# Down product of the second layer's MLP: tokens stationary, 512 columns of weights moving, in four groups of four units

## The chip, the cores and the metric

The kernel runs on one core of a Trainium2 chip. The metric is the device time of one execution in microseconds (us); lower is better. The engines are called as the profile calls them: PE is TensorE (matmuls; PEld is its weight load), DVE is VectorE, ACT is ScalarE, POOL is GpSimd, and SP is the queue that issues most transfers from memory.

## The reference

Two decoder layers over 512 tokens of width 1024. Each layer is RMS norm, attention with its input and output projections, residual, then RMS norm, an MLP and residual. Only the MLP of the second layer is touched:

```python
def squared_relu_mlp(h, w_up, w_down):
    u = jnp.einsum("bsd,df->bsf", h, w_up)
    return jnp.einsum("bsf,fd->bsd", jnp.square(jax.nn.relu(u)), w_down)

def reference(x, ...):
    for layer in range(DEPTH):
        ...
        h = rms_norm(x, g_mlp[layer])
        x = x + squared_relu_mlp(h, w_up[layer], w_down[layer])
    return x
```

All of it is float32: x is (1, 512, 1024), `w_up` 1024 x 4096 and `w_down` 4096 x 1024 in each layer.

## The kernel before, in words

**Precision.** Every float32 operand of a matmul is split into two parts, `hi` (a copy rounded to fp32r, made by ACT) and `lo` (the rest, a subtraction on DVE). A product is three matmuls: hi with hi, lo with hi, hi with lo (`mm3` and `mm_half`). So each 128x512 block of weights costs one ACT cast (`whi`, L763) and one DVE subtraction (`wlo`, L764) ahead of its matmuls.

**The MLP (function `mlp`, called with `last` for the second layer).** The 4096 hidden values are cut into 16 units of 256. An item ("U", u) computes unit u: four positions of 12 matmuls, each 128x512 (weights stationary, 512 tokens moving), then ReLU. After it `unit_end` squares the unit and prepares it for the down product.

**The down product.** It is done with seven block products in place of eight. The weights of an item are cut in quarters 11, 12, 21, 22 (first digit: half of the output columns, second digit: half of the hidden values), the activations in quarters b11 to b22 (half of the hidden values, half of the tokens). Sums of quarters (s1 to s4 of the weights, made in `ws`, L856; t1 to t4 of the activations, made in `t_sums`, L784) enter four of the products. `ORDER` lists them: (11, b11), (1, t1), (2, t2), (4, b22), (3, t3), (12, b21), (22, t4), with the PSUM bank X, Y or Z in which each is accumulated. An item ("D", g, dp) does all seven for group g of four units and for 256 output columns, so each group takes four items, dp 0 to 3, of 7 positions. A product is 4 x 3 matmuls with weights stationary and 256 tokens moving (L950, L953, L954), and one more matmul per item opens bank Y (L943). `combine` (L966) adds each bank to the residual `accs`, which lies with the channels on the partitions.

**The last unit.** In the second layer the fourth group holds three units (`NL = 1`), and unit 15 is done in `down_last` at the very end by plain products: 32 transposes bring `accs` into token order (L1109), ACT copies them scaled (L1113), then 48 matmuls with tokens stationary and 512 weight columns moving (L1118 to L1122), and DVE scales and adds (L1124) before the output is stored (L1125).

**The norm.** The MLP runs on activations that aren't normed yet. `mean_squares` forms v = mean of squares + eps in two layouts: along the free dimension (`ssum`, from a 128x512 matmul, L791) and along partitions (`r2col` = 1/v, L793). The residual is multiplied by v (`scale_residual`, eight DVE products, L799), and `down_last` multiplies everything by 1/v.

**The order.** The items stand in one list; each item is cut in positions, and at position n the loop issues the matmuls of n, `combine` of n-1, the cast of position n+6 (`prep`, R = 6; its subtraction follows one position later), the load of weights some positions further ahead (`early`), and whatever was put on that position by hand (`at`, `plan`, the tables FIN, FIND, FINL). Within the MLP the four engines' instructions are kept in this order (`PINS = 'pgva'`). There are 7 buffers each for `whi` and `wlo`, 4 for loaded weights (`wraw`, 512 KB each), 14 for split activations (`act`), and 4 + 4 PSUM banks (`pA`, `pB`). Items around a group: U(4g+4), then the four D items of group g, then U(4g+5) to U(4g+7).

Of the kernel before, what the change touches and what calls it, by code (L numbers as in the profile page):

```python
# [9 lines left out]
F32 = mybir.dt.float32  # L10
# [30 lines left out]
SCENG = ('vv', 'vv', 'vv', 'vv')  # L41
# [6 lines left out]
FINL = ((0, 0, 1, 1, 2), (8, 16, 16, 18, 20))  # L48
NL = 1
# [24 lines left out]
def trunk(ctx, tc, x, g_mix, g_mlp, w_in_even, a_q_gain, a_k_gain, b_q_gain, b_k_gain, b_sinks,  # L74
# [660 lines left out]
    def mlp(li, accs, attention_end, last):  # L735
# [5 lines left out]
        with ExitStack() as c2:  # L741
# [46 lines left out]
            def mean_squares():  # L788

                pr = bank("pB", "r2")  # L790
                tc.keep_in_program_order(nc.tensor.matmul(pr, ones, ssum, start=True, stop=True))  # L791
                if last:
                    vec(nc.vector.tensor_scalar(r2col, token_sums(ssum, True), 1.0 / D, EPS, op0=OP.mult, op1=OP.add))  # L793
                    vec(nc.vector.reciprocal(r2col, r2col))
                vec(nc.vector.tensor_scalar(ssum, pr, 1.0 / D, EPS, op0=OP.mult, op1=OP.add))
# [14 lines left out]
            NS = 3  # L810
            items = [("U", u) for u in range(4)]
            for g in range(NS):
                items.append(("U", 4 * g + 4))
                items += [("D", g, dp) for dp in range(4)]
                items += [("U", 4 * g + u) for u in range(5, 8)]
            items += [("D" if last else "E", NS, dp) for dp in range(4)]
            pos, first = [], []
            for j, it in enumerate(items):
                first.append(len(pos))
                pos += [(j, p) for p in range(7 if it[0] == "D" else 4)]  # L820
# [4 lines left out]
            def load(j):  # L825
                if j in raws or j >= len(items):
                    return
                it = items[j]
                raws[j] = [wp.tile([P, 4, 256], F32, tag="wraw", bufs=RAW, name="wraw") for _ in range(2)]
                for h in range(2):  # L830
                    if it[0] != "U":
                        src = wd[h, :, 4 * it[1]:4 * it[1] + nk(j), it[2] * 256:it[2] * 256 + 256]
# [3 lines left out]
                    nc.sync.dma_start(raws[j][h][:, :nk(j)], src)  # L836

            def nk(j):

                return 4 - NL if last and items[j][:2] == ("D", NS) else 4  # L840

            def quarter(j, q):
                return raws[j][q % 10 - 1][:, :nk(j), (q // 10 - 1) * P:(q // 10) * P]

            def ws(j, i):
# [5 lines left out]
                s = sums[j, i] = mp.tile([P, 4, P], F32, tag=f"s{i}", bufs=1, name="s")[:, :nk(j)]  # L851
# [13 lines left out]
            def early(n):  # L865

                if n < NP:
                    j, p = pos[n]
                    load(j)
                    if items[j][0] == "D" and ORDER[p][0] < 10:  # L870
                        ws(j, ORDER[p][0])

            def prep(n):
                if n >= NP:
                    return
                j, p = pos[n]
                if items[j][0] != "D":
# [6 lines left out]
                halves(hi[:, :nk(j)], lo[:, :nk(j)], src)  # L884
                ready[n] = hi, lo

            def up(j, p, hi, lo):

                if p % 2 == 0:
                    res[j, p] = bank(("pA", "pB")[j % 2], "up")  # L890
# [40 lines left out]
            def product(j, p, hi, lo):  # L931
# [13 lines left out]
                for k in range(nk(j)):  # L945
                    b = store[4 * it[1] + k][name]
                    mm_half(o, hi[:, k], lo[:, k], b, new and k == 0, k == nk(j) - 1, k == 0, not new)
# [20 lines left out]
            def unit_end(j):  # L968
# [8 lines left out]
                def whole(e):  # L977
                    s = slot("s") if u < 15 or last else mp.tile([P, 2, 512], F32R, tag="t24", bufs=2, name="s")
                    halves(s[:, 0], s[:, 1], v[:, e])
                    store[u, e] = s  # L980

                if last and u >= 16 - NL:
                    return [square, lambda: None, lambda: None, lambda: whole(0), lambda: whole(1)]
# [32 lines left out]

                return [square, tsum, b_part, lambda: t_part(0), lambda: t_part(1)]
# [6 lines left out]
            def plan(j):  # L1024
# [7 lines left out]
                else:  # L1032
                    offs = FINL[u - 15 + NL] if u >= 15 - NL else FIND if u % 4 == 0 and u else FIN
# [11 lines left out]
            for dp in range(4):  # L1045
                at(SCALE[dp], lambda dp=dp: scale_residual(dp, SCENG[dp]))
                if not last:
                    at(first[-7] + SC3[dp], lambda dp=dp: scale_residual(dp, "vv"))
            if not last:
                at(RPL, lambda: vec(nc.vector.reciprocal(ssum, ssum)))  # L1050

            def end(n):
# [3 lines left out]
                {"U": up_end, "D": combine, "E": direct_end}[items[j][0]](j, p)  # L1056
# [20 lines left out]
            for n, (j, p) in enumerate(pos):  # L1077
                early(n + R + LS)
                hi, lo = ready.pop(n)
                {"U": up, "D": product, "E": direct}[items[j][0]](j, p, hi, lo)  # L1080
# [11 lines left out]
            if last:  # L1092
                down_last(li, accs, [store[u, e] for u in range(16 - NL, 16) for e in range(2)], r2col)
# [3 lines left out]

    def down_last(li, accs, ss, r2col):

        r0 = FF // P - 2 * NL  # L1100
        for ch in range(2):
            cs = slice(ch * 512, (ch + 1) * 512)
            ws, rest = [], []
            for k in range(0, 2 * NL, 2):
                ws += load_w([(0, 0, w_down[li, (r0 + k) * P:(r0 + k + 2) * P, cs])], 512, 2, PAT_MLP)
            for m in range(4):
                pt = bank("pB", "fin")
                for c in range(4):
                    nc.tensor.transpose(pt[:, c * P:(c + 1) * P],  # L1109
                                        accs[2 * ch + c // 2][:, c % 2, m * P:(m + 1) * P], ident)  # L1110
                if m % 2 == 0:
                    rest.append(act.tile([P, 2, 512], F32, tag="act", name="rest"))
                nc.scalar.activation(rest[m // 2][:, m % 2], pt, AF.Copy, scale=r2col[:, m:m + 1])  # L1113
            for m in range(4):
                ts = slice(m * P, (m + 1) * P)
                o = bank("pA", "dn")
                for f in range(2 * NL):
                    mm = nc.tensor.matmul(o, ss[f][:, 0, ts], ws[f][0], start=f == 0, stop=False)  # L1118
                    if f == 0:
                        tc.keep_in_program_order(mm)  # L1120
                    nc.tensor.matmul(o, ss[f][:, 0, ts], ws[f][1], start=False, stop=False)
                    nc.tensor.matmul(o, ss[f][:, 1, ts], ws[f][0], start=False, stop=f == 2 * NL - 1)  # L1122
                a = rest[m // 2][:, m % 2]
                nc.vector.scalar_tensor_tensor(a, o, r2col[:, m:m + 1], a, op0=OP.mult, op1=OP.add)  # L1124
                nc.sync.dma_start(out[0, m * P:(m + 1) * P, cs], a)  # L1125
# [27 lines left out]
```

## Time and profile before

| what | value |
|---|---|
| median of 3 runs | 1192.4 us (1188.94 to 1193.04) |
| profiled execution, its time | 1192.98 us |
| span of its instructions | 1191.2 us, so 1.8 us lie around it |
| mean granted clock of TensorE | 0.995 of full |
| busy share: PE, DVE, ACT, POOL | 98%, 75%, 54%, 18% |
| MLP of the second layer | first matmul at 842.73 us, end at 1191.2 us |

A matmul's row shows when it started and its latency; matmuls are pipelined, so what one costs is the distance from its start to the next one's start.

### The profile page before, as it was taken

How to read it: one execution, taken by the hardware profiler on the slowest of the kernel's cores; microseconds unless marked ns; L12 is line 12 of the kernel's file. 1: busy time of each engine (PE TensorE's matmuls, PEld its weight loads, DVE VectorE, ACT ScalarE, POOL GpSimd, SP SyncE). 2: the span in 40 equal slices, each digit the busy share in tenths (PEclk: the TensorE clock that was granted, in tenths of full speed). 3: DMA queues.
4: the chain of work that ended last, by engine and by line, in shares of the span. 5: the costliest groups of instructions: out<-in, count | busy, mean ns of one | idle time of the engine just before them, and what ended most of it. 6: DMA issues, size and time to landing. Idle time of an engine off the chain costs nothing.

```text
span 1191.2 us, 18927 instructions
## 1 busy us (share of the span) xinstructions
PE 1162.3 (98%) x6902; PEld 1020.3 (86%) x6902; DVE 893.1 (75%) x1962; ACT 646.0 (54%) x1351; POOL 212.1 (18%) x307
## 2 busy tenths in 40 slices
PE   8799989999999999999999999999999999999998
PEld 7787887888888988988887888887889989889897
DVE  4987899878956947865657887878879578569585
ACT  6255876665445545444335675655655455455453
POOL 2445444200000000000155445432000000000000
PEclk9899999999999999999999999999999999999999
DMA  7342115232332332233443433343322423323322
GB/s 250 114 109 79 37 37 155 76 103 75 107 110 84 94 120 88 90 113 109 152 125 107 106 100 100 103 124 106 107 89 72 125 89 106 103 83 100 116 68 82
DMA packets 106197, 122.46 MB, mean 103 GB/s; under 512 B 6088, under 2 KB 95208, under 8 KB 106104
## 3 DMA queue, kind: packets, MB, share of 16 engines
q1 hardware_dynamic: 104920, 117.03, 32.3%
q0 software_dynamic: 576, 2.10, 0.5%
q10 hardware_dynamic: 608, 2.13, 0.4%
q8 instruction: 54, 0.88, 0.3%
q14 instruction: 39, 0.32, 0.1%
HBM read 108.10 MB, written 6.32 MB: 96 GB/s over the span
## 4 chain that ended last, share of the span: by engine, by line
PE 81%; DVE 10%; DMA 3%; issue 2%; ACT 2%; POOL 1%; SPq 0%; ACTq 0%; POOLq 0%; DVEq 0%
PE up L165 10%; PE up L168 10%; PE up L169 10%; PE pj L232 4%; PE pj L234 4%; PE pj L233 4%; PE Y L950 3%; PE Y L953 3%; PE Y L954 3%; PE O L383 2%; PE Z L950 2%; PE X L953 2%; PE X L950 2%; PE Z L954 2%; PE Z L953 2%; PE X L954 2%
## 5 line engine op out<-in xcount | busy, mean ns | idle before, releaser
L165 PE MATMUL up<-xin,whi 128*128 128x512 f32 x512 | 199.8, 390 | 0.0
L168 PE MATMUL up<-xin,wlo 128*128 128x512 f32 x512 | 199.3, 389 | 0.0
L169 PE MATMUL up<-xin,whi 128*128 128x512 f32 x512 | 199.2, 389 | 0.0
L763 ACT CAST whi<-wraw 128x512 fp32r<-128x512 f32 (+1 forms) x228 | 138.7, 613 | 106.4 <-PE up L169 48.3
L764 DVE TENSOR_TENSOR wlo<-wraw,whi 128x512 fp32r<-128x512 f32 (+1 forms) x228 | 152.1, 679 | 56.5 <-ACT whi L763 54.3
L169 PEld LDWEIGHTS up<-xin,whi 128*128 128x128 f32 x512 | 96.1, 188 | 20.1
L165 PEld LDWEIGHTS up<-xin,whi 128*128 128x128 f32 x512 | 96.1, 188 | 20.0 <-issue 0.2
L168 PEld LDWEIGHTS up<-xin,wlo 128*128 128x128 f32 x512 | 96.1, 188 | 19.9 <-issue 0.2
L763 ACT CAST whi<-s 128x512 fp32r<-128x512 f32 (+1 forms) x112 | 67.6, 604 | 70.0 <-PE Y L954 35.0
L343 ACT ACTIVATE P<-P,negm 128x128 f32<-128x128 f32 (+5 forms) x128 | 69.5, 544 | 52.9 <-DVE negm L340 51.0
L950 PE MATMUL Y<-t,whi 128*128 128x256 f32 x324 | 92.7, 286 | 3.0 <-DVE acc L966 2.6
L901 ACT ACTIVATE u<-up 128x512 f32<-128x512 f32 x64 | 38.3, 598 | 99.7 <-PE up L169 99.7
L953 PE MATMUL Y<-t,wlo 128*128 128x256 f32 x324 | 91.7, 283 | 0.0
L954 PE MATMUL Y<-t,whi 128*128 128x256 f32 x324 | 91.6, 283 | 0.0
L153 POOL TENSOR_SCALAR whi<-wraw 128x512 fp32r<-128x512 f32 x96 | 65.8, 687 | 140.7 <-PE pj L234 118.3
L232 PE MATMUL pj<-whi,hn 128*128 128x512 f32 (+2 forms) x256 | 88.7, 346 | 0.0
L234 PE MATMUL pj<-whi,hn 128*128 128x512 f32 (+2 forms) x256 | 86.9, 339 | 0.0
L233 PE MATMUL pj<-wlo,hn 128*128 128x512 f32 (+2 forms) x256 | 86.8, 339 | 0.0
L764 DVE TENSOR_TENSOR wlo<-s,whi 128x512 fp32r<-128x512 f32 (+1 forms) x112 | 73.7, 663 | 2.4 <-ACT whi L763 2.4
L232 PE MATMUL pj<-whi,h 128*128 128x512 f32 (+1 forms) x192 | 68.5, 361 | 6.9 <-DVE v L161 3.1
L156 POOL TENSOR_TENSOR wlo<-wraw,whi 128x512 fp32r<-128x512 f32 x52 | 69.7, 1344 | 21.8 <-ACT whi L151 18.7
L234 PE MATMUL pj<-whi,h 128*128 128x512 f32 (+1 forms) x192 | 66.6, 348 | 0.0
(200 smaller groups left out, 3138.6 us busy)
## 6 DMA issues: line engine op xcount, KB each, us to landing
wraw<-in_w_up SPq DMA_DIRECT2D x64, 512.0 KB, 3.8
wraw<-in_w_down SPq DMA_DIRECT2D x58, 512.0 KB, 4.0
wraw<-in_w_in_odd SPq DMA_DIRECT2D x36, 256.0 KB, 3.0
K<-K SPq DMA_DIRECT2D x26, 256.0 KB
wraw<-in_w_in_even SPq DMA_DIRECT2D x10, 512.0 KB, 4.4
wraw<-in_w_in_even SPq DMA_DIRECT2D x16, 256.0 KB, 4.4
xl<-xsp SPq DMA_DIRECT2D x8, 512.0 KB
bias<-csp SPq DMA_DIRECT2D x16, 256.0 KB, 3.5
```

Of the source, the lines that this page charges most:

```text
L156: in_order((nc.gpsimd if lo == "pool" else nc.vector).tensor_sub(dst_l, src, dst_h.bitcast(F32)))
L165: m = nc.tensor.matmul(o, wh, xh, start=start, stop=False, skip_group_check=more)
L168: nc.tensor.matmul(o, wl, xh, start=False, stop=False, skip_group_check=more)
L169: nc.tensor.matmul(o, wh, xl, start=False, stop=stop, skip_group_check=more)
L232: nc.tensor.matmul(o, xh, hi[:, :n], start=k == 0, stop=False)
L233: nc.tensor.matmul(o, xh, lo[:, :n], start=False, stop=False)
L234: nc.tensor.matmul(o, xl, hi[:, :n], start=False, stop=k == DC - 1)
L763: sca(nc.scalar.copy(dst_h, src))
L764: late.append(lambda: vec(nc.vector.tensor_sub(dst_l, src, dst_h.bitcast(F32))))
L950: m = nc.tensor.matmul(o, wh, b(0), start=start, stop=False, skip_group_check=more)
L953: nc.tensor.matmul(o, wl, b(0), start=False, stop=False, skip_group_check=more)
L954: nc.tensor.matmul(o, wh, b(1), start=False, stop=stop, skip_group_check=more)
```

## The change

In the second layer alone, the down product is turned round. An item ("T", g) now does group g for all 1024 output columns: a weight quarter is 512 columns wide, and the products have 128 tokens stationary and 512 weight columns moving. Each of the seven products has four positions (one for each unit k of the group), and a position is 2 token blocks x 3 matmuls of 128x512. Result banks hold tokens on the partitions, so `combine_t` adds a bank, multiplied by `r2col`, to `rest`, the residual in token order. The 32 transposes for `rest` move from the end to positions 11 to 18 (in U2 to U4), four at each position, unscaled. The fourth group takes all four units, with unit 15's preparation put right behind it (`FIN15`), and `down_last` is gone, as are `scale_residual` and the 128x512 matmul of `mean_squares` in this layer. Weights come in pieces of 2 x 512 columns; quarters 21 and 22 have four buffers of their own (`mraw`), their sums are formed in place there, and quarter 22 is loaded a second time for the last product (key 220). In the very last product all matmuls of token block 0 stand ahead of those of block 1.

```diff
-SCENG = ('vv', 'vv', 'vv', 'vv')
...
-FINL = ((0, 0, 1, 1, 2), (8, 16, 16, 18, 20))
-NL = 1
+FIN15 = (0, 0, 1, 3, 5)
+REST = 11
...
-                pr = bank("pB", "r2")
-                tc.keep_in_program_order(nc.tensor.matmul(pr, ones, ssum, start=True, stop=True))
                 if last:
                     vec(nc.vector.tensor_scalar(r2col, token_sums(ssum, True), 1.0 / D, EPS, op0=OP.mult, op1=OP.add))
                     vec(nc.vector.reciprocal(r2col, r2col))
+                    return
+                pr = bank("pB", "r2")
...
+            for g in range(4):
+                if g < 3:
+                    items.append(("U", 4 * g + 4))
+                if last:
+                    items.append(("T", g))
+                else:
+                    items += [("D" if g < 3 else "E", g, dp) for dp in range(4)]
+                if g < 3:
+                    items += [("U", 4 * g + u) for u in range(5, 8)]
...
+                pos += [(j, p) for p in range({"D": 7, "T": 28}.get(it[0], 4))]
...
+            LOADS = {-2: 11, -1: 21, 0: 22, 6: 12, 16: 220}
+
+            def load_t(n):
...
+                    for kp in range(2):
+                        if q in (11, 12, 220):
+                            r = wp.tile([P, 2, 512], F32, tag="wraw", bufs=RAW, name="wraw")
+                        else:
+                            r = mp.tile([P, 2, 512], F32, tag="mraw", bufs=4, name="mraw")
+                        k = 4 * it[1] + 2 * kp
+                        nc.sync.dma_start(r, wd[e, :, k:k + 2, d * 512:d * 512 + 512])
+                        raws[j, q, kp] = r
+
+            def sums_t(n):
+
+                if n >= NP or items[pos[n][0]][0] != "T" or pos[n][1] % 2:
+                    return
...
+                a11, a12, a21, s = (raws.get((j, q, kp)) for q in (11, 12, 21, 22))
+                if i == 1:
+                    vec(nc.vector.tensor_add(s, a21, s))
+                elif i == 2:
+                    vec(nc.vector.tensor_sub(s, s, a11))
+                elif i == 3:
+                    vec(nc.vector.tensor_sub(a21, a11, a21))
+                elif i == 4:
+                    vec(nc.vector.tensor_sub(s, a12, s))
...
+            def product_t(j, p, hi, lo):
...
+                if p == 2:
+                    res[j, "Y"] = [bank("pA", "Y") for _ in range(2)]
...
+                def block(b, k, hi, lo):
+                    s = store[4 * items[j][1] + k][name]
+                    o = res[j, bk][b]
+                    sh, sl = (s(part)[:, b * P:(b + 1) * P] for part in range(2))
+                    m = nc.tensor.matmul(o, sh, hi, start=new and k == 0, stop=False, skip_group_check=not new)
+                    pin("p", m)
+                    nc.tensor.matmul(o, sh, lo, start=False, stop=False, skip_group_check=not new)
+                    nc.tensor.matmul(o, sl, hi, start=False, stop=k == 3, skip_group_check=not new)
...
+            def combine_t(j, p):
+
+                if p % 4 != 3:
+                    return
...
+                    vec(nc.vector.scalar_tensor_tensor(a, o, r2col[:, m:m + 1], a, op0=OP.mult, op1=OP.add))
+                    if j == len(items) - 1 and i in (4, 3, 12, 22):
+                        nc.sync.dma_start(out[0, m * P:(m + 1) * P, e * 512:e * 512 + 512], a)
...
+            def rest_T(n):
...
+                pt = bank("pB", "rT")
+                for c in range(4):
+                    pin("p", nc.tensor.transpose(pt[:, c * P:(c + 1) * P],
+                                                 accs[2 * e + c // 2][:, c % 2, m * P:(m + 1) * P], ident))
+                sca(nc.scalar.copy(rest[e, t][:, b], pt))
...
+                if u == 15:
+                    return [square, b_part, tsum, lambda: t_part(0), lambda: t_part(1)]
...
+                for n in range(8):
+                    at(REST + n, lambda n=n: rest_T(n))
...
+                sums_t(n + R + 1)
...
-                down_last(li, accs, [store[u, e] for u in range(16 - NL, 16) for e in range(2)], r2col)
```

Up to the second layer's MLP the instructions of every engine stand as before. Three places where they don't:

On PE, at the start of the down product of group 1, before the change: the first item opens bank Y and then does the first product, whose stationary operand is `whi` or `wlo` and whose moving operand is a 256-token slice of a `b` tile.

```order
5213 L943 MATMUL Y<-b_10223,whi 128x256
5214 L950 MATMUL X<-b_10223,whi 128x256
5215 L953 MATMUL X<-b_10223,wlo 128x256
5216 L954 MATMUL X<-b_10223,whi 128x256
5217 L950 MATMUL X<-b_10729,whi 128x256
```

The same place now:

```order
5057 L1013 MATMUL X<-whi,b_10204 128x512
5058 L1015 MATMUL X<-wlo,b_10204 128x512
5059 L1016 MATMUL X<-whi,b_10204 128x512
5060 L1013 MATMUL X<-whi,b_10204 128x512
5061 L1015 MATMUL X<-wlo,b_10204 128x512
5062 L1016 MATMUL X<-whi,b_10204 128x512
```

Where a unit had three matmuls of 256 columns per item, it now has six of 512 columns per group, three for each token block, and the openers of Y come two positions later.

On DVE, in the middle of group 0 before the change (`s` are sums of weight quarters, `wlo` the subtractions, `t` the sums of unit 4's activations):

```order
1441 L966 TENSOR_TENSOR acc_0_8856<-Z,acc_0_8856 128x256
1442 L764 TENSOR_TENSOR wlo<-wraw,whi 128x512
1443 L856 TENSOR_TENSOR s<-wraw 128x512
1444 L966 TENSOR_TENSOR acc_0_8856<-Y,acc_0_8856 128x256
1445 L764 TENSOR_TENSOR wlo<-s,whi 128x512
1446 L784 TENSOR_TENSOR t<-u 128x256 x2
1447 L784 TENSOR_TENSOR t<-u,t 128x256 x2
1448 L966 TENSOR_TENSOR acc_0_8856<-Z,acc_0_8856 128x256
```

And now:

```order
1430 L763 TENSOR_TENSOR wlo<-mraw,whi 128x512 x2
1431 L871 TENSOR_TENSOR mraw<-mraw,wraw 128x1024
1432 L763 TENSOR_TENSOR wlo<-mraw,whi 128x512
1433 L783 TENSOR_TENSOR t<-u 128x256 x2
1434 L783 TENSOR_TENSOR t<-u,t 128x256 x2
1435 L763 TENSOR_TENSOR wlo<-mraw,whi 128x512
1436 L875 TENSOR_TENSOR mraw<-wraw,mraw 128x1024
1437 L763 TENSOR_TENSOR wlo<-mraw,whi 128x512 x2
1438 L875 TENSOR_TENSOR mraw<-wraw,mraw 128x1024
1439 L763 TENSOR_TENSOR wlo<-mraw,whi 128x512
1440 L1042 SCALAR_TENSOR_TENSOR rest<-Z,r2col,rest 128x512 x2
```

The sums are now 1024 wide and stand close together in the first half of a group, and the additions of banks come in pairs of 512, once every four positions.

On SP, the loads of the second layer's MLP up to the second group, before the change:

```order
107 L836 DMA wraw<-in_w_up 128x4x256 x8
108 L836 DMA wraw<-in_w_down 128x4x256 x8
109 L836 DMA wraw<-in_w_up 128x4x256 x8
110 L836 DMA wraw<-in_w_down 128x4x256 x8
111 L836 DMA wraw<-in_w_up 128x4x256 x8
```

And now:

```order
111 L839 DMA wraw<-in_w_up 128x4x256 x5
112 L857 DMA wraw<-in_w_down 128x2x512 x4
113 L857 DMA mraw<-in_w_down 128x2x512
114 L857 DMA wraw<-in_w_down 128x2x512
115 L857 DMA mraw<-in_w_down 128x2x512
116 L857 DMA wraw<-in_w_down 128x2x512
117 L857 DMA mraw<-in_w_down 128x2x512 x2
118 L839 DMA wraw<-in_w_up 128x4x256 x8
```

A group now loads ten pieces of 512 KB in place of eight, and the `mraw` pieces of the next group stand in the queue between and behind the second loads of quarter 22, ahead of the next units' weights.

## Rows read from the trace of the kernel before

**Rows 1.** The page: engine totals, granted clock in 40 slices, last chain by engine.

```profile
PE 1162.3 (98%) x6902; PEld 1020.3 (86%) x6902; DVE 893.1 (75%) x1962; ACT 646.0 (54%) x1351; POOL 212.1 (18%) x307
...
PEclk9899999999999999999999999999999999999999
...
PE 81%; DVE 10%; DMA 3%; issue 2%; ACT 2%; POOL 1%; SPq 0%; ACTq 0%; POOLq 0%; DVEq 0%
```

**Rows 2.** Stretches of the second MLP; counts include instructions reaching in from neighbours.

```profile
core 0: us, PE busy (x) PEld busy (x) DVE busy (x) ACT busy (x) POOL busy (x), PEclk, DMA share, GB/s
...
898.92:939.95 41.03, 41.03 (x342) 40.89 (x341) 34.47 (x68) 21.79 (x39) 0.00 (x0) 1.00 0.33 103
939.95:983.49 43.54, 43.54 (x194) 36.04 (x193) 26.16 (x48) 22.11 (x41) 0.00 (x0) 1.00 0.31 97
...
1141.77:1172.64 30.87, 30.87 (x258) 30.78 (x256) 27.24 (x61) 17.30 (x35) 0.00 (x0) 1.00 0.23 74
1172.64:1174.30 1.66, 1.66 (x18) 1.66 (x17) 0.42 (x1) 1.02 (x2) 0.00 (x0) 1.00 0.00 0
1174.30:1179.86 5.56, 5.56 (x28) 4.55 (x26) 2.25 (x3) 1.40 (x3) 0.00 (x0) 1.00 0.25 94
...
1181.52:1187.07 5.55, 5.55 (x27) 4.41 (x25) 2.25 (x3) 1.40 (x3) 0.00 (x0) 1.00 0.38 142
1187.07:1191.20 4.13, 0.15 (x1) 0.00 (x0) 0.75 (x1) 0.00 (x0) 0.00 (x0) 0.83 0.34 127
```

**Rows 3.** PE in order of time, end of group 0 (start us, latency us).

```profile
939.71 0.28 PE L953 MATMUL Y<-t,wlo 128*128 128x256 f32 x1
939.83 0.28 PE L954 MATMUL Y<-t,whi 128*128 128x256 f32 x1
```

**Rows 4.** PE in order of time: mean of squares, and the start of the tail.

```profile
872.65 1.02 PE L791 MATMUL r<-ssum,ones 128*128 128x512 f32 x2
873.50 0.95 PE L605 MATMUL pc<-ones,ssum 128*128 128x1 f32 x8
...
1172.64 1.91 PE L1109 MATMUL fin<-ident,acc 128*128 128x128 f32 x16
...
1174.30 0.48 PE L1118 MATMUL dn<-whi,s 128*128 128x512 f32 x1
...
1174.62 0.40 PE L1121 MATMUL dn<-wlo,s 128*128 128x512 f32 x1
...
1174.85 0.39 PE L1122 MATMUL dn<-whi,s 128*128 128x512 f32 x1
```

**Rows 5.** Groups by form in the second MLP (busy us, mean ns, idle before).

```profile
L764 DVE TENSOR_TENSOR wlo<-wraw,whi 128x512 fp32r<-128x512 f32 x97 | 65.3, 685 | 28.6 <-ACT whi L763 28.6
L763 ACT CAST whi<-wraw 128x512 fp32r<-128x512 f32 x97 | 59.7, 619 | 50.8 <-PE up L169 23.3 <-PE Y L954 15.0 <-PE X L954 7.4
...
L856 DVE TENSOR_TENSOR s<-wraw 128x512 f32<-128x512 f32 x24 | 16.4, 683 | 0.0
...
L784 DVE TENSOR_TENSOR t<-u,t 128x256 f32<-128x256 f32 x30 | 12.7, 423 | 0.5
...
L1124 DVE SCALAR_TENSOR_TENSOR rest<-dn,r2col,rest 128x512 f32<-128x512 f32 x8 | 6.0, 750 | 8.8 <-PE dn L1122 8.8
```

**Rows 6.** DVE in order of time within group 0.

```profile
906.99 0.42 DVE L966 TENSOR_TENSOR acc<-Y,acc 128x256 f32<-128x256 f32 x1
907.32 0.68 DVE L764 TENSOR_TENSOR wlo<-s,whi 128x512 fp32r<-128x512 f32 x1
907.92 0.42 DVE L966 TENSOR_TENSOR acc<-X,acc 128x256 f32<-128x256 f32 x1
```

**Rows 7.** Weight tile of the second MLP and DMA issues: landing times.

```profile
DMA to landing us min/median/max: 3.1/3.8/4.9
...
q1 hardware_dynamic: 104920, 117.03, 32.3%
```

More of the change, by code (lines that the diff above doesn't have):

```diff
@@ L825, in load @@
             def load(j):
-                if j in raws or j >= len(items):
+                if j in raws or j >= len(items) or items[j][0] == "T":
                     return
@@ L876, in prep @@
                 j, p = pos[n]
+                if items[j][0] == "T":
+                    i = {1: 22, 2: 22, 3: 21, 4: 22, 22: 220}.get(ORDER[p // 4][0], ORDER[p // 4][0])
+                    hi = wp.tile([P, 512], F32R, tag="whi", bufs=NHI, name="whi")
+                    lo = wp.tile([P, 512], F32R, tag="wlo", bufs=NLO, name="wlo")
+                    halves(hi, lo, raws[j, i, p % 4 // 2][:, p % 2])
+                    ready[n] = hi, lo
+                    return
                 if items[j][0] != "D":
@@ L889, in up @@
                 if p % 2 == 0:
-                    res[j, p] = bank(("pA", "pB")[j % 2], "up")
+                    res[j, p] = bank(("pA", "pB")[items[j][1] % 2 if last else j % 2], "up")
                 o = res[j, p - p % 2]
@@ L944, in product @@
                     pin("p", m)
-                for k in range(nk(j)):
+                for k in range(4):
                     b = store[4 * it[1] + k][name]
-                    mm_half(o, hi[:, k], lo[:, k], b, new and k == 0, k == nk(j) - 1, k == 0, not new)
+                    mm_half(o, hi[:, k], lo[:, k], b, new and k == 0, k == 3, k == 0, not new)
+            def product_t(j, p, hi, lo):
+                i, k = divmod(p, 4)
+                _, name, bk = ORDER[i]
+                new = (j, bk) not in res
+                if new:
+                    res[j, bk] = [bank("pB" if bk == "Z" else "pA", bk) for _ in range(2)]
+                    res[j, bk, "new"] = i
+                new = res[j, bk, "new"] == i
+                s = store[4 * items[j][1] + k][name]
+                if p == 2:
+                    res[j, "Y"] = [bank("pA", "Y") for _ in range(2)]
+                    res[j, "Y", "new"] = None
+                    for o in res[j, "Y"]:
+                        pin("p", nc.tensor.matmul(o, s(0)[:, :P], hi, start=True, stop=True))
+                def block(b, k, hi, lo):
+                    s = store[4 * items[j][1] + k][name]
+                    o = res[j, bk][b]
[4 more added lines that the diff above has]
+                    nc.tensor.matmul(o, sl, hi, start=False, stop=k == 3, skip_group_check=not new)
+                if j == len(items) - 1 and i == 6:
+                    res["end", k] = hi, lo
+                    block(0, k, hi, lo)
+                    if k == 3:
+                        for kk in range(4):
+                            block(1, kk, *res["end", kk])
+                else:
+                    for b in range(2):
+                        block(b, k, hi, lo)
@@ new lines, in mlp @@
+            rest = {}
+            def rest_T(n):
+                e, t, b = n // 4, n // 2 % 2, n % 2
+                if b == 0:
+                    pool_, tag, bufs = {(0, 0): (act, "act", 14), (0, 1): (mp, "rest", 1)}.get((e, t), (act, "acc", 4))
+                    rest[e, t] = pool_.tile([P, 2, 512], F32, tag=tag, bufs=bufs, name="rest")
+                m = 2 * t + b
+                pt = bank("pB", "rT")
[3 more added lines that the diff above has]
+                sca(nc.scalar.copy(rest[e, t][:, b], pt))
@@ L1044, in mlp @@
             at(SQ[-1], mean_squares)
-            for dp in range(4):
-                at(SCALE[dp], lambda dp=dp: scale_residual(dp, SCENG[dp]))
-                if not last:
+            if last:
+                for n in range(8):
+                    at(REST + n, lambda n=n: rest_T(n))
+            else:
+                for dp in range(4):
+                    at(SCALE[dp], lambda dp=dp: scale_residual(dp, "vv"))
                     at(first[-7] + SC3[dp], lambda dp=dp: scale_residual(dp, "vv"))
-            if not last:
                 at(RPL, lambda: vec(nc.vector.reciprocal(ssum, ssum)))
```

76 lines of the change are left out of this document (29 added, 47 removed).

## The prediction, made before the run

> **What bounds the kernel now.** I first read the page's totals [rows 1]: PE is busy 98% of the span, no other engine over 75%, and the last chain runs through PE for 81%. A busy share says nothing of a single stage, so I cut the second MLP into stretches at the starts of its PE work [rows 2]. In every stretch up to 1187.07 us PE is busy from end to end, at a granted clock of 1.00, while DVE is busy 34.47 of 41.03 us in a group of the down product and ACT 21.79. So in this stage the number of PE instructions times the distance between their starts is the time; after the last matmul comes a tail of 4.13 us (last addition on DVE, last store).
>
> The distances come from the same stretches. A group of four D items has 4 x (1 + 7 x 12) = 340 matmuls and takes 41.03 us: 0.1207 us each, which the starts confirm (939.71, 939.83) [rows 3]; the 0.28 us of such a row is latency and no price. The next stretch, four U items of 48 matmuls with 512 columns, takes 43.54 us: 0.2268 each [rows 2]. Matmuls with tokens stationary and 512 weight columns moving exist already in the tail: 48 of them take 5.56 + 5.55 us, 0.231, with starts 0.23 apart (1174.62, 1174.85) [rows 2, 4]. So a matmul of 512 columns costs less than two of 256 (0.2414): the fixed part of each is spread over more columns.
>
> **What the change removes and adds on PE.** The trace has every kind that is added, so the sum goes by its rows.
>
> Groups 0 to 2. A T item has 7 x 4 x 6 = 168 matmuls of 512 columns and two openers of Y: 170 x 0.2268 = 38.6 us in place of 41.03. Three groups: -7.3 us.
>
> Group 3 and unit 15. Before, three units took 30.87 us and unit 15's 48 matmuls 11.11 us [rows 2], 41.98 together; now one T item of 38.6 us: -3.4 us.
>
> Transposes. The 32 stay and cost PE the same 2 x 1.66 us [rows 2]. What changes is that they go in eight lots of four between matmuls, not in two of 16. The first matmul after a lot started its successor 0.32 us later in place of 0.23 (1174.30 to 1174.62) [rows 4], so each lot costs some 0.09 us more: +0.7 us. The copies of `rest` move to ACT in U2 to U4, where it is busy for half of a U stretch [rows 2].
>
> Mean of squares. The 128x512 matmul leaves PE: 872.65 to 873.50, -0.85 us [rows 4].
>
> The tail behind the last matmul keeps its parts: one addition of 0.75 us [rows 5] and one store of the same size. That block 0 of the last product is finished first lets its addition and store lie beside block 1's matmuls; at the end one addition and one store remain, as before: 0.
>
> Sum: -7.3 - 3.4 + 0.7 - 0.85 = -10.8 us, if nothing makes PE wait. The profiled execution took 1192.98 us (1191.2 of span and 1.8 around it) and comes to 1182.2; it stands 0.6 us over the median of the runs, which comes to 1181.6. I forecast 1182.
>
> A rule of the Trainium skill speaks against this ("TensorE: Matmul & The Clock Gate", Back-to-back issue gap): a warm matmul follows the one before after its columns at 2.4 GHz plus 2.5 ns, 109 ns for 256 columns and 216 for 512. By it the whole conversion would give 3.0 us and not 10.7; the distances of 121 and 227 ns in the rows above don't agree with it, and the measurement decides.
>
> **What hides the rest.** DVE. By starts, a 512 operation takes 0.60 us of DVE and a 256 one 0.33 (907.32 to 907.92, 906.99 to 907.32) [rows 6], so 1024 columns, which no row shows, cost 1.14 by the same slope; bounds are 0.60 (width free) and 1.20 (two of 512). A bank addition with `r2col` takes 0.75 in its row against 0.68 for a plain operation [rows 5], so 0.67 by starts. A T group then needs 28 x 0.60 for `wlo`, 8 x 1.14 for sums, 12 x 0.67 for banks and 3.5 for the next unit's preparation (four t sums, one 256 and three 512 subtractions): 37.4 us under 38.6 of PE. On the average it is hidden, barely. The first half is the tight one, since the sums crowd there: up to the 12th position 12 x 0.60 + 6 x 1.14 + 1.3 (t sums) + 0.9 (b parts) + 1.3 (one pair of banks) = 17.5 us, while PE needs 12 x 1.36 + 0.45 = 16.8. DVE falls 0.7 us behind there, with `wlo` prepared five positions (6.8 us) ahead, and the bank that PE writes again at position 12 free about 3 us early. The eight products of `scale_residual` leave DVE; they were hidden.
>
> ACT has the same 28 casts as before, at 0.62 us [rows 5] less than half of a group. Two places are thin. In group 0 the 14 `act` buffers don't do: units 0 to 3 hold twelve, `rest` one, unit 4's b2 one, so the cast of its t1 (position 12) waits in ACT's order until unit 0's t1 tile is read last, at position 16; behind it stands the cast for position 19. PE then has positions 17 and 18 left, 2.7 us, and ACT and DVE need two casts' and two subtractions' pipeline, about 2.0: 0, or up to 1 us once. In group 3 unit 15's preparation follows its last matmul directly: ReLU, one cast, two squares and b11's cast at 0.6 each and a subtraction make 3.4 us, and PE gets there after 3 x 1.36 us; its t1, needed at position 7 after 10.0 us, is ready after about 9.9 by the same adding up. 0 to 1 us; I take 0 for both.
>
> SP. Landing takes 3.1 to 4.9 us [rows 7]. From position 9 to 22 of a group ten pieces of 0.524 MB are asked for (two of quarter 22 again, four `mraw` of the next group, four of the next units): 5.2 MB in 17.7 us, 296 GB/s. The queue moved 117.03 MB in 32.3% of the span [rows 7], 304 GB/s when it moves, so this stretch is nearly full. The second piece of quarter 22 has nine positions (12 us), with three pieces ahead of it (6.9 us in all); the first U weights behind the group about five (6.8 us), and then six prepared positions of cover. I take 0; up to 1.5 us a group.
>
> **Rivals.**
> 1. Small waits add up: group 0's buffer, unit 15, a late first weight piece. 2 to 4 us: 1184 to 1186.
> 2. Weights late in every group but the last, 1.5 to 2 us each beyond the cover: about 1188. For it: the nearly full stretch; against: the landings so far.
> 3. DVE becomes the bound. If nothing of its operations overlaps (each waits for ACT or PE), durations count: 28 x 0.685 + 8 x 1.22 + 12 x 0.75 + 4.2 = 42.2 us a group, 3.6 over PE, 14.4 in all: 1196.6, slower than before. It decides once DVE needs more than 38.6 us a group. Against: it sits at 84% now and its rows overlap wherever they follow each other.
> 4. The change doesn't do what it says: 512 columns cost twice 256, 0.2414 as two starts of D, so a T group takes 41.03 again, and 1.0 us is left: 1191.9. The tail's own matmuls of this very form [rows 4] speak against it. The gap rule of the Trainium skill named above points the same way (ratio 1.98); the trace's ratio is 1.88.
> 5. Slower by the clock: the lots of transposes among U2 to U4 bring the granted clock to its lower level, half. Eight positions of 3.1 us would take 25 us more: 1207. It decides if PEclk of 15 to 40 us behind the MLP's start shows under 1.00. Against: two lots of 1.66 us without any matmul show 1.00, and so do the stretches after them [rows 2]. The Trainium skill (same page, PE-mode transpose) says that transposes don't count as TensorE being busy; the trace shows no fall from lots four times as long.
>
> **How the numbers follow.** No wait that shows: 0.71, 1180 to 1184 with the spread of runs. Rival 1: 0.13. Rival 2: 0.05. Rival 3: 0.05. Rival 4: 0.03. Rival 5: 0.03. The first two hold 0.84 and reach 1186; the spread of the runs before (1188.94 to 1193.04) adds some 2 us at both ends, and rival 2 lies just behind: 1179 to 1188. A measurement of this kernel can tell about 0.5%, 6 us, from no change: under 1186.4 is faster (0.71 + 0.13, less a little where waits join: 0.83), rivals 2 to 4 are the same (0.13), rival 5 and larger stalls slower (0.04).
>
> **What would show it.** Right: PE busy end to end again from 842.7 us on; starts 0.227 apart in the T items and each item about 38.6 us long; the last matmul some 10.8 us earlier, 4.1 us before the end; DVE over 95% busy within a group. Wrong: a gap in PE behind position 12 of a group with `wlo` or a bank as its releaser (DVE), behind position 18 of group 0 (buffer), at position 3 or 7 of group 3 (unit 15), at the first U item behind a group (weights); distances near 0.24; a clock under 1.00.

## The result, and the profile after

The changed kernel takes 1179.84 us (median of 6 runs, 1177.5 to 1182.01) where the kernel before takes 1191.95 (median of 6, 1188.94 to 1194.19): ratio 0.9899, 95% interval 0.988 to 0.9918, so 9.8 to 14.3 us less. The forecast was 1182, a gain of 10.8 us, range 1179 to 1188; the median lies 2.2 us under it, near the lower end. The profiled execution took 1180.63 us, with a span of 1178.9.

The page of the kernel after: totals, granted clock and last chain, beside [rows 1].

```profile
PE 1151.4 (98%) x6256; PEld 986.0 (84%) x6256; DVE 883.2 (75%) x1867; ACT 643.5 (55%) x1341; POOL 212.4 (18%) x307
...
PEclk9899999999999999999999999999999999999999
...
PE 82%; DVE 9%; DMA 3%; issue 2%; ACT 2%; POOL 1%; SPq 0%; POOLq 0%; ACTq 0%; DVEq 0%
```

The shares are those of before. What moved is seen only in the stretches of the second MLP: up to and with the column sums, the eight lots of transposes, group 0, three U items, group 1, and at the end group 3 and the tail. They answer to [rows 2].

```profile
core 0: us, PE busy (x) PEld busy (x) DVE busy (x) ACT busy (x) POOL busy (x), PEclk, DMA share, GB/s
841.68:871.60 29.92, 29.92 (x133) 24.77 (x132) 20.94 (x38) 19.63 (x36) 0.00 (x0) 1.00 0.36 119
871.60:875.23 3.63, 3.63 (x22) 3.10 (x21) 2.13 (x5) 0.62 (x1) 0.00 (x0) 1.00 0.13 47
875.23:900.80 25.57, 25.57 (x129) 21.20 (x128) 14.21 (x25) 16.60 (x32) 0.00 (x0) 1.00 0.12 42
900.80:939.33 38.53, 38.53 (x171) 31.91 (x170) 34.81 (x54) 20.12 (x37) 0.00 (x0) 1.00 0.46 138
939.33:982.85 43.52, 43.52 (x193) 36.04 (x192) 25.92 (x46) 22.56 (x42) 0.00 (x0) 1.00 0.29 96
982.85:1021.39 38.54, 38.54 (x172) 31.91 (x170) 34.23 (x52) 21.38 (x37) 0.00 (x0) 1.00 0.50 153
...
1136.08:1174.77 38.69, 38.69 (x171) 31.72 (x169) 31.32 (x47) 17.24 (x31) 0.00 (x0) 1.00 0.22 75
1174.77:1178.90 4.13, 0.01 (x1) 0.00 (x0) 0.75 (x1) 0.00 (x0) 0.00 (x0) 1.00 0.17 63
```

PE is busy from end to end again, at a granted clock of 1.00, and PE's view of waits has no row from 842 us on. A group takes 38.53 us in place of 41.03; 38.53 / 170 is 0.2267 us a matmul. From the first matmul of the MLP to the end of the span it was 348.47 us before (842.73 to 1191.20) and is 337.22 now (841.68 to 1178.90): 11.25 less. The other 1.05 us of the difference of the spans lie ahead of the MLP, where both kernels have the same instructions; in eleven profiles of kernels that are the same up to there the MLP began anywhere from 840.68 to 843.30. So the experiments below are read by stretches of the MLP, which repeat to some hundredths, and the whole times only beside them. Where no number of runs is given, a kernel ran once.

DVE in order of time in group 0, and PE where it takes up bank Y again at position 16 (start us, latency us). Y is two banks, one for each token block: the first of the two additions (0.75 us each) frees the one that PE takes up first, the second the one that it takes up three matmuls later.

```profile
919.50 1.41 DVE L1042 SCALAR_TENSOR_TENSOR rest<-Y,r2col,rest 128x512 f32<-128x512 f32 x2
```

```profile
923.01 0.39 PE L1013 MATMUL Y<-whi,t 128*128 128x512 f32 x1
```

And the same group on ACT: the cast that the prediction saw waiting for a free `act` buffer, and what stands behind it.

```profile
919.09 0.62 ACT L762 CAST whi<-mraw 128x512 fp32r<-128x512 f32 x1 [1.20 <-DVE mraw L873]
924.57 0.62 ACT L762 CAST t<-t 128x512 fp32r<-128x512 f32 x1 [4.86 <-PE Y L1016]
925.10 0.61 ACT L762 CAST whi<-mraw 128x512 fp32r<-128x512 f32 x1
```

The first bank is free at 920.25, 2.8 us before PE needs it; in groups 1 and 2 it is the same (group 1: free at 1002.30, needed at 1005.07), and in group 3 it is 1.8 (1156.45, 1158.29). The second bank has the same time to spare in each group. The `t` cast stood 4.86 us until PE was through with unit 0's tile. The cast behind it ended at 925.71, its subtraction at 926.53, and PE read that `wlo` at 927.32: 0.79 us to spare.

### The profile page after: what moved, and what is told of

The parts are those of the page before. It is cut to its first block, busy times and chain, and to the rows that moved or that the text cites. A ratio compares the mean times of both kernels' runs of the same rounds, so it can differ in the third digit from the quotient of the medians.

```text
span 1178.9 us, 17505 instructions
## 1 busy us (share of the span) xinstructions
PE 1151.4 (98%) x6256; PEld 986.0 (84%) x6256; DVE 883.2 (75%) x1867; ACT 643.5 (55%) x1341; POOL 212.4 (18%) x307
## 4 chain that ended last, share of the span: by engine, by line
PE 82%; DVE 9%; DMA 3%; issue 2%; ACT 2%; POOL 1%; SPq 0%; POOLq 0%; ACTq 0%; DVEq 0%
PE up L164 10%; PE up L168 10%; PE up L167 10%; PE pj L231 4%; PE pj L233 4%; PE pj L232 4%; PE O L382 3%; PE PT L362 2%; PE op L168 2%; PE Y L1016 2%; PE Y L1015 2%; PE Y L1013 2%; PE op L164 2%; PE op L167 2%; PE Y L1062 1%
## 5 line engine op out<-in xcount | busy, mean ns | idle before, releaser
L762 ACT CAST whi<-wraw 128x512 fp32r<-128x512 f32 x228 | 139.3, 619 | 105.6 <-PE up L168 47.9
L763 DVE TENSOR_TENSOR wlo<-wraw,whi 128x512 fp32r<-128x512 f32 x228 | 151.7, 686 | 53.7 <-ACT whi L762 53.4
L783 DVE TENSOR_TENSOR t<-u 128x256 f32<-128x256 f32 x56 | 23.2, 424 | 63.3 <-ACT u L1087 61.5
L232 PE MATMUL pj<-wlo,h 128*128 128x512 f32 (+1 forms) x192 | 66.2, 345 | 0.0
L350 POOL TENSOR_SCALAR P<-P,rden 128x256 f32<-128x256 f32 (+2 forms) x96 | 46.9, 491 | 92.0 <-DVE rden L345 91.4
L374 ACT CAST PT<-PT 128x256 fp32r<-128x256 f32 (+3 forms) x128 | 49.4, 405 | 19.1 <-PE PT L362 18.3
L155 DVE TENSOR_TENSOR wlo<-wraw,whi 128x512 fp32r<-128x512 f32 (+1 forms) x68 | 46.4, 691 | 16.9 <-POOL whi L152 10.6
```

The lines of the kernel that those rows point to most:

```text
L155: in_order((nc.gpsimd if lo == "pool" else nc.vector).tensor_sub(dst_l, src, dst_h.bitcast(F32)))
L232: nc.tensor.matmul(o, xh, lo[:, :n], start=False, stop=False)
L374: nc.scalar.copy(dst[:, 0], pt[:, :n])
L762: sca(nc.scalar.copy(dst_h, src))
L763: late.append(lambda: vec(nc.vector.tensor_sub(dst_l, src, dst_h.bitcast(F32))))
```

## The experiments

### Width of the moving operand: 256 and 128 columns

The theory: each matmul costs a distance between starts, and 512 columns are cheaper than two times 256. The rival: the gain comes from the rest of the change (order, unit 15, a shorter end), not from the width.

```diff
-m = nc.tensor.matmul(o, sh, hi, ...)
-nc.tensor.matmul(o, sh, lo, ...)
-nc.tensor.matmul(o, sl, hi, ...)
+for st, mv in ((sh, hi), (sh, lo), (sl, hi)):
+    for c in range(0, 512, 256):      # 128 in the second kernel
+        m = nc.tensor.matmul(o[:, c:c + 256], st, mv[:, c:c + 256], ...)
```

> The changed kernel, but each 512-column matmul of the T items is issued as two of 256 columns (336 a group in place of 168, the two openers of Y stay). Theory (the distance between matmul starts is a fixed part plus columns, as the 0.1207 and 0.2267 us of the two traces): 336 x 0.1207 + 0.45 = 41.0 us a group in place of 38.53, +2.5 each, +9.9 in all, about 1189.8 us. Rival (the gain came from the new order, from unit 15 within the group and the shorter tail, not from the width): groups stay at 38.5 to 38.9, about 1180. By the Trainium skill's back-to-back gap (page TensorE: Matmul & The Clock Gate, 2.5 ns a matmul) it would be +0.42 us a group, 1.7 in all.

> The same with four matmuls of 128 columns (672 a group). Theory A (fixed part plus columns; the line through 0.1207 at 256 and 0.2267 at 512 has 14.7 ns + 0.414 ns a column, so 0.0677 at 128): 672 x 0.0677 + 0.45 = 46.0 us a group, about 1210 us. Theory B (each matmul brings its own weight load, and below some width the load sets the distance; in the groups of before the load rows fill 40.89 of 41.03 us, and transposes of 128 columns stood 0.104 apart): 672 x 0.104 to 0.12 = 70 to 81 us a group, 1306 to 1350 us.

Groups 0 and 1 with 256 columns, by stretches:

```profile
901.48:942.24 40.76, 40.76 (x340) 40.67 (x339) 35.11 (x54) 20.78 (x37) 0.00 (x0) 1.00 0.45 136
985.78:1026.54 40.76, 40.76 (x339) 40.66 (x338) 34.73 (x52) 21.67 (x37) 0.00 (x0) 1.00 0.47 147
```

And with 128:

```profile
901.06:976.52 75.46, 75.46 (x676) 75.36 (x674) 36.79 (x54) 21.31 (x37) 0.00 (x0) 1.00 0.27 84
```

With 256 columns a group is 40.76 us, 2.23 more than with 512, in all four; the MLP takes 346.14 us (842.36 to 1188.50) and the kernel 1190.19 (median of 10, ratio 0.998 to the kernel before, 0.9965 to 0.9996). Nothing but the width differs from the changed kernel: it alone is worth 8.9 of the 11.25 us of the MLP, and the rival is left with the other 2.3. The back-to-back rule of the Trainium skill that the expectation quotes ("TensorE: Matmul & The Clock Gate", Back-to-back issue gap) would make it 1.7, and the 8.9 measured don't agree. The Trainium skill gives that formula there for an isolated matmul and says that in a stream of weight loads and matmuls both set the spacing; the matmuls here are such a stream.

With 128 columns the kernel takes 1328.94 us. Less the two openers, 75.46 us hold 672 matmuls: 0.1116 us each, where the line through the other two widths gave 0.0677. Theory B was right: below some width the distance no longer falls with the columns. Even the eight matmuls with one moving column at the column sums [rows 4] start 0.112 apart from the second on.

That the weight load is the reason is likely, but argued. The load rows (second engine column) fill 75.36 of 75.46 us here and 31.91 of 38.53 with 512 columns; but they fill 40.67 of 40.76 with 256 as well, where the distance is longer, so a full column alone doesn't tell. The starts say more: with 256 columns each load starts 2 ns behind the start of a matmul, with 128 the loads start 0.112 apart without a break and the matmuls follow them. No run has a matmul without its load, which would settle it.

The Trainium skill ("TensorE: Matmul & The Clock Gate", LDWEIGHTS (loading the stationary operand)) gives a weight load its 128 columns at 1.2 GHz; that makes an estimate of 107 ns a load, and the 112 ns of these rows lie 5% above it.

### Uneven pieces: 320 and 192 columns

The same edit, with each matmul cut at column 320.

```diff
+        for c, d in ((0, 320), (320, 512)):
+            m = nc.tensor.matmul(o[:, c:d], st, mv[:, c:d], ...)
```

> The changed kernel with each 512-column matmul of the T items as one of 320 and one of 192. Theory A (below some width the weight load sets the distance, about 0.112 as with 128 columns; above it the distance is columns / 2.4 GHz + some 14 ns): 0.147 + 0.112 = 0.259 a pair, 168 x 0.259 + 0.45 = 43.9 us a group, +5.4 each, about 1201.5. Theory B (columns + 14 ns holds down to 192, and only 128 is slower): 0.147 + 0.094 = 0.241, 40.9 us a group, +2.4 each, about 1189.5.

```profile
901.40:945.29 43.89, 43.89 (x339) 43.80 (x338) 35.38 (x54) 20.95 (x37) 0.00 (x0) 1.00 0.42 138
```

43.89 us a group (1202.88 us in all): a pair costs (43.89 - 0.45) / 168 = 0.2586 us. The same columns in two equal halves cost 2 x (40.76 - 0.45) / 336 = 0.240. This is theory A, which had 43.9: 0.147 for 320 columns and 0.112, the same as for 128, for 192. The rows bear out the sum, not the parts:

```profile
989.79 0.25 PE L1016 MATMUL X<-whi,b 128*128 128x192 f32 x1
989.88 0.43 PE L1016 MATMUL X<-wlo,b 128*128 128x320 f32 x2
990.15 0.33 PE L1016 MATMUL X<-whi,b 128*128 128x320 f32 x1
```

A matmul starts 0.088 us behind one of 192 columns and 0.171 behind one of 320, while the loads start 0.109 and 0.151 apart by turns: no load follows another by less than some 0.11. So 256 columns (0.120) stand just above the floor, and cutting a matmul as 320 and 192 is worse than in halves.

### How much room DVE has

The prediction put DVE's need at 37.4 us a group under 38.53 of PE. One more addition of 512 columns, whose result nobody reads, at every fourth position, and in a second kernel at every second:

```diff
+if items[j][0] == "T" and p % 4 == 0:      # p % 2 in the second kernel
+    ...
+    vec(nc.vector.tensor_add(spare[1], spare[0], spare[0]))
 prep(n + R)
```

> The changed kernel with one more DVE addition of 512 columns (result unused) at every fourth position of the T items: 7 a group, 4.2 us of DVE by starts. Theory A (the prediction's sum: a group needs 37.4 us of DVE, so 1.2 us of slack): +3.0 us a group, about 12 in all, 1191 to 1192. Theory B (from the trace after: DVE busy 34.2 of 38.5 us, and each wlo is ready 3.1 us or more ahead of its matmul in groups 1 and 2; by the tightest position three of the seven, 1.8 us, have run): no stall in groups 1 to 3; in group 0, where the wlo of position 19 is ready only 0.79 us ahead, 0 to 1 us. 1179 to 1181.

> The same at every second position: 14 a group, 8.4 us of DVE. Theory A: 8.4 - 1.2 = 7.2 us a group, 29 in all, 1207 to 1209. Theory B: by the tightest positions (17 to 21) six to eight have run, 3.6 to 4.8 us against leads of 3.1 to 4.2: 0.5 to 1 us a group in groups 1 to 3, 1 to 2.5 in group 0, 1182 to 1185.

Groups 0, 1 and 3 with 7 additions:

```profile
901.62:940.15 38.53, 38.53 (x171) 31.91 (x170) 37.65 (x59) 19.95 (x36) 0.00 (x0) 1.00 0.42 134
983.67:1022.21 38.54, 38.54 (x172) 31.91 (x170) 37.52 (x59) 20.99 (x37) 0.00 (x0) 1.00 0.45 138
...
1136.90:1175.60 38.70, 38.70 (x171) 31.73 (x169) 35.09 (x54) 17.03 (x31) 0.00 (x0) 1.00 0.22 75
```

And with 14, with the waits of PE over the whole MLP (total us, times, longest), and PE and DVE where the first of them falls:

```profile
901.93:941.63 39.70, 39.09 (x172) 31.76 (x170) 39.56 (x63) 19.93 (x36) 0.00 (x0) 1.00 0.41 126
985.15:1024.01 38.86, 38.86 (x171) 31.75 (x170) 37.91 (x60) 20.07 (x36) 0.00 (x0) 1.00 0.42 128
...
1139.00:1178.97 39.97, 39.06 (x171) 31.57 (x169) 39.10 (x61) 17.03 (x31) 0.00 (x0) 1.00 0.19 66
```

```profile
PE Y L1013 <- DVE rest L1042: 1.5, 2, 0.9
...
924.92 0.47 PE L1013 MATMUL Y<-whi,t 128*128 128x512 f32 x1 [0.61 <-DVE rest L1042]
...
924.03 1.41 DVE L1042 SCALAR_TENSOR_TENSOR rest<-Y,r2col,rest 128x512 f32<-128x512 f32 x2
```

4.2 us of DVE more a group cost nothing at all (1181.45 us; the MLP takes 337.2 us as without them). 8.4 us cost 1.2, 0.3, 0.3 and 1.3 us in the four groups, 3.1 in all (1184.89 us). Theory A, the slack by the prediction's sum, called for 12 and 29 us and falls; the room is what theory B read from the trace after. The wait that came first is not one for `wlo` but for the first addition of bank Y, ahead of position 16, the place with 2.8 us to spare in the trace after (1.8 in group 3). Six of the 14 extra additions stand ahead of it, 3.6 us. They make it 3.4 us later in group 0, where PE then waits 0.61 us, and 2.9 in group 3, where it waits 0.91; in groups 1 and 2 idle time of DVE takes up so much that it is 2.6 later, and PE doesn't wait there. With seven, three stand ahead of it, 1.8 us, and no group waits. Most of the rest of the loss in groups 0 to 2 lies at position 24, where PE takes up bank Y once more. The expectation had the sum right (2.5 to 5.5 us by its terms, 3.1 measured), but not groups 1 to 3 (0.5 to 1 us each), and it looked in the wrong place: it watched the `wlo` of positions 17 to 21 alone.

### The transposes in two lots

```diff
-at(REST + n, lambda n=n: rest_T(n))
+at((9, 17)[n // 4], lambda n=n: rest_T(n))
```

> The changed kernel with the 32 transposes in two lots of sixteen (positions 9 and 17) in place of eight lots of four. Theory (a lot costs its transposes and a fixed start behind them; in the trace after, eight lots with the matmuls behind them take 3.80 us more than the matmuls alone, and sixteen in a row took 1.66 in the trace before): 2 x (1.66 + 0.06) = 3.44, so the stretch from the column sums to the first T item is 0.36 us shorter, 28.8 in place of 29.2; the end 1179.5. Rival (lots without matmuls lower the granted clock, the prediction's fifth rival, or four copies in a row on ACT make PE wait): the stretch is longer, by 1 us or more, or its granted clock under 1.00.

The two lots, and the U matmuls between and behind them:

```profile
867.89:869.55 1.66, 1.66 (x17) 1.66 (x16) 0.00 (x0) 1.03 (x3) 0.00 (x0) 1.00 0.85 269
869.55:892.32 22.77, 22.77 (x108) 18.95 (x106) 13.64 (x27) 13.57 (x27) 0.00 (x0) 1.00 0.21 73
892.32:893.98 1.66, 1.66 (x17) 1.66 (x16) 0.50 (x1) 1.03 (x3) 0.00 (x0) 1.00 0.00 0
893.98:899.52 5.54, 5.54 (x27) 4.59 (x26) 4.08 (x7) 4.42 (x10) 0.00 (x0) 1.00 0.01 3
```

From its first matmul (840.68) to the end of the span (1177.6) the MLP takes 336.92 us, 0.30 less than with eight lots (0.36 expected), and the granted clock is 1.00 in and behind both lots. So the lots cost what their number of restarts (the late second start behind each lot) says, and nothing by the clock; 1179.37 us in one run.

### Without the openers of bank Y

```diff
-for o in res[j, "Y"]:
-    pin("p", nc.tensor.matmul(o, s(0)[:, :P], hi, start=True, stop=True))
```

> The changed kernel without the two openers of bank Y in each T item (the bank's earlier matmuls have written all of it). Theory (PE is bound by the number of its instructions, each costs its distance and nothing else is hidden in it): 170 to 168 matmuls a group, 38.53 - 0.45 = 38.08 us, 1.8 in all, about 1178. Rival (DVE or ACT sets the pace of a group, PE would only wait there): groups stay at 38.5.

```profile
982.70:1020.78 38.08, 38.08 (x170) 31.53 (x168) 34.21 (x52) 21.30 (x37) 0.00 (x0) 1.00 0.48 152
```

Each group is 0.45 us shorter, two matmuls, and the MLP takes 335.32 us (841.98 to 1177.3), 1.9 less. So each PE instruction taken out here is time, and the rival falls.

### Unit 15 outside the fourth group

This undoes one part of the change: group 3 with three units, and unit 15 by 48 plain matmuls behind it.

```diff
+if last:
+    items.append(("V", 3))
...
-FIN15 = (0, 0, 1, 3, 5)
+FIN15 = (3, 3, 3, 9, 13)
...
+for m in range(4):
+    sh, sl = (store[15, p % 2][:, part, m * P:(m + 1) * P] for part in range(2))
+    o = res[j, p - p % 2][m]
+    pin("p", nc.tensor.matmul(o, sh, hi, start=p % 2 == 0, stop=False))
+    nc.tensor.matmul(o, sh, lo, start=False, stop=False)
+    nc.tensor.matmul(o, sl, hi, start=False, stop=p % 2 == 1)
```

> The changed kernel with unit 15 taken out of group 3 again: a T item of three units, and behind it 48 plain matmuls of 512 columns for unit 15. It undoes that part of the change alone. Theory (only the count of matmuls matters): 128 + 48 in place of 170, (176 - 170) x 0.2267 = +1.4 us: 29.0 + 10.9 = 39.9 in place of 38.69; about 1181. Rival (unit 15's chain of preparations costs something in group 3 that the rows hide, or the longer tail of stores costs more): the difference is under 0.7, or over 2.5.

> Unit 15 outside group 3 as in the run before it, with the sums of weight quarters in the three-unit item one step later in the order (there they had overwritten a quarter that was still to be read). Theory as there: group 3 and unit 15 together 29.0 + 10.9 to 11.1 = 39.9 to 40.1 us in place of 38.69, the tail 4.1 again. Rival: under 39.4 or over 41.2.

The first of the two kernels forms a sum of weights over a quarter that is still to be read, so what it computes is not the MLP; its times alone are used. The second kernel, by stretches: three units, unit 15, the tail.

```profile
1135.62:1165.21 29.59, 29.31 (x130) 23.95 (x128) 25.67 (x39) 14.72 (x27) 0.00 (x0) 1.00 0.20 63
1165.21:1176.07 10.86, 10.86 (x49) 8.82 (x47) 5.83 (x9) 0.00 (x0) 0.00 (x0) 1.00 0.28 104
1176.07:1180.20 4.13, 0.18 (x1) 0.00 (x0) 0.97 (x2) 0.00 (x0) 0.00 (x0) 1.00 0.63 235
```

29.59 + 10.86 = 40.45 us in place of 38.69, 1.8 more, and 0.35 over what was expected: the three-unit item has one start 0.44 us late, behind a cast of ACT. In the first of the two kernels that item took 29.01 us, the count alone, which makes 39.87, 1.2 more (expected 1.4), and the kernel 1183.48 us (1181.98 for the second); its MLP began at 843.30 and that of the second at 841.22, which makes up the difference. So taking unit 15 into the seven products is worth 1.2 to 1.8 us, where the count of matmuls has 1.4. By the first kernel, the rest of the 3.3 us that group 3 and unit 15 gave together is 1.9 for the width of the three units (30.87 to 29.01) and 0.25 for unit 15's matmuls, which take 10.86 in place of 11.11 without transposes between them.

### Transposes in two lots, no openers in either layer

> The changed kernel with the transposes in two lots, and without the openers of bank Y in both layers (8 matmuls of 512 columns, 12 of 256). Theory: -0.36 - 1.81 - 12 x 0.1207 = -3.6 us, about 1176.2, ratio to the kernel before 0.9868. Rival (the openers' time is given back in waits for the copy of bank X into Y): 1178 to 1180, 0.989 to 0.990.

It takes 1178.03 us (median of 4, 1175.67 to 1178.89), ratio 0.9884 to the kernel before (0.9867 to 0.99). The interval overlaps that of the changed kernel, and the median lies at the lower end of what the rival had, so the whole times alone don't decide. The second MLP takes 335.08 us (838.82 to 1173.90) in place of 337.22, 2.1 less, about the 0.3 and 1.9 of the two experiments. In the first layer it is otherwise. Its three groups with openers, in the changed kernel:

```profile
292.81:337.95 45.14, 42.76 (x342) 42.45 (x340) 37.76 (x69) 21.80 (x39) 0.00 (x0) 0.96 0.31 95
381.50:422.53 41.03, 41.03 (x341) 40.89 (x340) 34.47 (x68) 21.80 (x39) 0.00 (x0) 1.00 0.35 103
466.08:508.26 42.18, 41.67 (x341) 41.05 (x340) 34.27 (x65) 20.88 (x37) 0.00 (x0) 1.00 0.34 101
```

And without them:

```profile
292.61:336.46 43.85, 41.15 (x337) 40.50 (x336) 37.66 (x69) 21.63 (x39) 0.00 (x0) 1.00 0.32 97
380.01:420.69 40.68, 40.67 (x338) 40.40 (x337) 34.46 (x68) 21.64 (x39) 0.00 (x0) 1.00 0.34 104
464.23:506.17 41.94, 41.28 (x338) 40.58 (x337) 34.22 (x65) 20.88 (x37) 0.00 (x0) 1.00 0.33 101
```

Four openers are 0.48 us a group, and 0.35 and 0.24 come in the second and third. In the first, the 1.29 hold a change of the clock: PE waits 2.4 us there for an addition of DVE, with and without openers. In nine of the eleven traces in which this layer is the same, the granted clock falls to 0.50 behind that wait (302.00 to 304.00 us in the changed kernel's trace), and the group takes 44.9 to 45.1 us; in the other two it stays at 1.00, as here, and the group takes 44.2. Against those, this group gives some 0.4. So the first layer gives about 1.0 us of 1.45, and both layers 3.1 of 3.6. The rival is there in part: in the third group PE's wait for the copy of bank X into Y is 0.51 us in place of 0.39, longer by just the 0.12 of an opener.

## Why the prediction was right

**What bounds the stage.** It said that the number of PE instructions times their distance is the time. Half the width moved the second MLP by 8.9 us where 9.9 were expected by that product, the openers by 1.9 where 1.8 were, and unit 15 by 1.2 to 1.8 where 1.4 were; added DVE work did not move it until 4.2 us a group were passed.

**The sum.** -10.8 us were forecast and -11.25 measured within the MLP. Groups 0 to 2: -7.3 forecast, 3 x 2.5 = -7.5 measured. Group 3 and unit 15: -3.4, measured 41.98 to 38.69, -3.3. Eight lots: +0.7 forecast from the restart of [rows 4], +0.5 measured (25.57 us less 96 x 0.2267 and the 3.32 of the transposes). Mean of squares: -0.85, and the stretch up to the column sums is 0.86 shorter. Tail: 4.13 both times, 0. The U items between the groups take 43.52 us in place of 43.54, in all 0.1 that the sum left out. The medians lie 12.1 us apart; what the two traces differ by beyond the MLP's 11.25 us lies ahead of it, where the kernels are the same.

**The two thin places.** Both are where it put them, and both held. In group 0 the cast of unit 4's t1 waited for position 16; it left 0.79 us. In group 3 unit 15's t1 was forecast for 9.9 us of 10.0; it was ready at 1145.12, after 9.0, and PE reached position 7 at 1146.05, 0.9 us to spare. Both margins are under the 1 us that the prediction allowed for either place, so that neither cost anything was luck in part.

**Rival 1** (small waits) and **rival 2** (weights late) cost PE nothing. The late weights are there, though, behind group 0:

```profile
ACT whi L762 <- DMA wraw<-in_w_up: 4.5, 3, 2.3
```

Three casts of U weights waited 4.5 us in all for their transfers; the positions prepared ahead covered them, and groups 1 and 2 have no such row. **Rival 4** (512 costs twice 256) falls with the first experiment: 0.2267 against 2 x 0.120, a ratio of 1.89. The back-to-back rule of the Trainium skill ("TensorE: Matmul & The Clock Gate", Back-to-back issue gap) that the prediction named beside it had 1.98; it is the formula for an isolated matmul there, a condition that the prediction left out. **Rival 5** (clock): 1.00 with eight lots and with two.

**What was off: DVE.** "DVE over 95% busy within a group" did not come: 34.2 to 34.8 of 38.53 us, 89 to 90%. The prices were right (in group 1, 1024 columns stood 1.143 us apart where 1.14 was worked out, bank additions 0.66 where 0.67 was). The step that failed is setting the whole need of 37.4 us against PE's own 38.6: two of the eight sums run ahead of PE's group and two of the bank additions behind it (2 x 1.14 + 2 x 0.66 = 3.6 us), where DVE has time. And the prediction judged the room by position 12, with bank Z some 3 us early (4.3 measured in groups 0 to 2, 2.4 in group 3); the tightest bank is Y: four positions later 2.8 us early, in group 3 1.8, and in group 0 1.8 at position 24 too (first addition ended at 932.12, PE there at 933.89). **Rival 3**, which set durations against PE's time (42.2 us), erred in the same way and further: it would begin only with more than 4.2 us of DVE a group on top, and with 8.4 us it is a matter of 0.3 to 1.3 us a group.

## What to carry to other kernels

Where PE is busy end to end and each matmul brings its own weight load, turn a product so that the moving operand is as wide as a bank, and count instructions times the distance of their starts, from rows of that width in the same kernel. Judge the engine beside it not by a busy share or by a sum a group, but by how early its result is there at the tightest place, the free bank as well as the prepared weights; a few useless instructions of a known length measure that room directly. Where PE does wait, as in the first layer, an instruction taken out ahead of the wait gives less than its price.

## What the runs showed of the hardware

The distance of matmul starts with a weight load of 128 columns for each, at a granted clock of 1.00 (the level of 2.4 GHz): 0.2267 us for 512 columns and 0.120 for 256, but 0.112 for 128 and for a single column. A pair of 320 and 192 takes 0.259, as it would with 0.147 for the 320, by the line through 512 and 256, and 0.112 for the 192. So the distance falls with the width down to about 256 columns and then stands. That line would have 0.068 for 128.

Behind one and the same wait of PE of 2.4 us, the granted clock fell to 0.50 (the level of 1.2 GHz) in nine of eleven traces and stayed at 1.00 in two; the group in which this happened was 0.7 to 0.9 us longer for it.
